# The first column block's sample tile: three products over 64 doubled columns, or two over high and low parts side by side

## The chip, the cores and the metric

The kernel runs on one core of one Trainium2 chip. The metric is the device time of one execution in microseconds (us). The engines are TensorE (PE, its weight loads PEld), VectorE (DVE), ScalarE (ACT), GpSimd (POOL) and SyncE (SP), which issues most transfers; ScalarE issues some too.

## The reference

One step of a decoder layer for 1024 prompt tokens and 64 sample tokens (8 sequences of 8), model width 1024. What matters here is its beginning, the normed input and the input projection, of which `gv` is one part of 768 columns:

```python
h = rmsnorm(x, norm_mix)
q, k, v, gu, gv, ga, gb = split_in(h @ w_in)
...
vn = layernorm(jax.nn.gelu(gv), ln_g, ln_b)
s = spatial_gating(jax.nn.gelu(gu), vn, ws, bs)
```

Attention, the gated merge, the ConvFFN and the final norm follow; the change leaves them alone. All tensors are float32.

## The kernel before

A float32 product is made of reduced-precision matmuls: each operand is split into a high part (a cast on ScalarE, or a scaled copy, L40 and L44) and a low part (the rest, on VectorE, L41 and L45), and a product is high x high + high x low + low x high, three matmuls into one PSUM bank.

The tokens lie in two groups. Group 0 has the 64 samples and the first 512 prompt tokens, 576 columns; group 1 the other 512. At the start, x of group 0 comes in 8 slices of 128 rows (k = 0 to 7, tiles `xk`, named `wh` and `wl` in the profile). `h_of` scales slice k by the norm's gain and splits it into `hs[k]`, a high and a low tile of 128x576. These lie in room that later belongs to the tiles `th` and `tl` of group 0, so the profile calls them so. The row's reciprocal root mean square is applied later, when PSUM is read: the squares of the slices (L637) are added up in `rs` (L639), the column sums come from five small matmuls (L476, in `stats`), and VectorE and GpSimd make the reciprocal root `rst` of them.

The weight blocks `gv0`, `gv1`, `v`, `gv2` are 256 columns wide, as `w2h` and `w2l`, with two buffers each: `v` can be cast only when `gv0` has been used. For `gv0` the five token tiles (samples, and four of 128 prompt tokens) have a PSUM bank each (`ps5`), and the loop runs over k outside and tiles inside, so that TensorE can start when the first slices have come. `mm_tok` makes a tile's three matmuls of one k: 128 token columns of `hs[k]` are the stationary operand, 256 weight columns the moving one. The sample tile takes columns 0 to 127 as well, of which only the first 64 are samples.

For the later blocks the sample tile is made otherwise. GpSimd copies the 64 sample columns of the high and of the low part of each k side by side into `pair_s` (L645), 128 columns, and two matmuls per k (L597) give high x w in rows 0 to 63 of the bank and low x w in rows 64 to 127. `joined` then copies the lower half to SBUF on ScalarE (L538) and adds the upper half on VectorE (L539). `gv_out` applies gelu with the row scale and stores the result; the `tokens` function runs a block and does one job of other preparation behind each tile.

A scheduler orders the instructions of each engine when the program is built; it takes the code's order and its own estimate of when each operand is there. What stands in the trace is that order. The names in it carry a buffer's number: `st_290` is the sample tile's bank of `gv0`, `st_291` to `st_294` the other four, `th3_249` holds `pair_s`.

Of the kernel before, what the change touches and what calls it, by code (L numbers as in the profile page):

```python
# [15 lines left out]
P = 128  # L16
D = 1024
KD = 8
# [16 lines left out]
def layer(tc, a):  # L35
# [11 lines left out]
    with ExitStack() as top:  # L47
# [311 lines left out]
        with ExitStack() as ph1:  # L359
# [158 lines left out]
            def h_of(k, x):  # L518
                hh, hl = rows576[2 * k], rows576[2 * k + 1]
                for s in (slice(0, 320), slice(320, 576)) if k == 0 else (slice(0, 576),):  # L520
                    scale_split(hh[:, s], hl[:, s], x[:, s], gains[:, 0, k:k + 1])
                hs.append((hh, hl))
# [5 lines left out]
            def mm_tok(ps, g, lo, w, k):  # L528
                wh, wl = w
                ah, al = ((part1(t, k, lo) for t in txa[1][k % 4]) if g else (t[:, lo:lo + P] for t in hs[k]))  # L530
                for i, (u, v) in enumerate(((ah, wh), (ah, wl), (al, wh))):
                    PE.matmul(ps, u, v[:, k, :], start=k + i == 0,  # L532
                              stop=k == KD - 1 and i == 2)

            def joined(ps):

                t = gvp.tile([P, 256], F32, name="gv")[0:NS]
                S.copy(t, ps[NS:P])  # L538
                V.tensor_add(t, t, ps[0:NS])  # L539
                return t  # L540
# [35 lines left out]
            def gv_out(g, i, p3, ps, v=None):  # L576
                name = groups[g]["toks"][i][0]
                m = NS if name == "s" else P
                if name == "s" and p3:
                    v = ps = joined(ps)  # L580
                elif v is None:
                    v = gvp.tile([P, 256], F32, name="gv")
                S.activation(v[0:m], ps[0:m], AF.Gelu_apprx_tanh, scale=1.0 if g else rstg[g][0:m, i:i + 1])
                nc.scalar.dma_start(gvd[name][0:m, 256 * p3:256 * p3 + 256], v[0:m])

            def tokens(g, key, out, jobs, new=True, after=None):
                if new:
                    W.get()
                    W.get()
                for i, (name, lo) in enumerate(groups[g]["toks"]):  # L590
                    ps = bank()[:, :256]
                    for k in range(KD):
                        if name != "s":
                            mm_tok(ps, g, lo, wide[key], k)
                            continue
                        for e in range(2):
                            PE.matmul(ps, pair_s[:, k], wide[key][e][:, k, :], start=k + e == 0,  # L597
                                      stop=k == KD - 1 and e == 1)
                    if after and i == 0:
                        after()  # L600
                    out(i, ps)
                    if jobs:
                        jobs.pop(0)()
# [18 lines left out]
                PE.matmul(ps[:, 0:P], ones, ones, start=True, stop=True)  # L622
            bank5 = [bank() for _ in toks0]
            ps5 = [x[:, :256] for x in bank5]
            W.split_part(0, 0, 2)
            for k, x in enumerate(xk):
                h_of(k, x)
                for part in ([(1, 0, 2)], [(0, 2, 4), (1, 2, 4)], [],
                             [(0, 4, KD), (1, 4, KD)], [], [], [], [])[k]:
                    W.split_part(*part)  # L630
                for kx in () if k == 0 else (0, 1) if k == 1 else (k,):
                    for i, (_, lo) in enumerate(toks0):
                        mm_tok(ps5[i], 0, lo, wide["gv0"], kx)
            W.load(5)
            W.emit(4)
            for k, x in enumerate(xk):
# [2 lines left out]
                    V.tensor_add(rsg[0], xk[0] if k == 1 else rsg[0], x)  # L639
            with tc.issue_after(dma.ins):  # L640
                load_late()
            pair_s = txa[0][3][0].rearrange("p j c -> p (j c)")[:, 0:KD * P].rearrange("p (k c) -> p k c", c=P)
            for k, x in enumerate(hs):
                for e in range(2):
                    G.tensor_copy(pair_s[:, k, 64 * e:64 * e + 64], x[e][:, 0:NS])  # L645
            rows, first_gv = {}, []

            def stats_first():
# [1408 lines left out]
```

## Time and profile before

| | |
|---|---|
| time, median of 3 runs | 1507.48 us (1507.39 to 1508.54) |
| profiled execution | 1506.67 us, span 1504.8 us |
| TensorE | 1491.9 us busy, 99% of the span, 12166 matmul records |
| VectorE, ScalarE, GpSimd | 77%, 55%, 19% of the span |
| granted TensorE clock | 0.998 |

A row of the timeline gives start, length, engine, line, operation, what it writes and reads, shapes, a count, and in brackets how long the engine was idle before it and what ended that. TensorE's matmuls overlap, and the profile models their ends: the pace is read from the starts. A weight load (PEld) that waits for its operand shows as a gap between two loads.

### The profile page before, as it was taken

To read this page: it belongs to the slowest core of one execution; us is meant where nothing else is said; L and a number is where in the kernel's file an instruction comes from. 1 tells how busy PE (TensorE), PEld (TensorE's weight loads), DVE (VectorE), ACT (ScalarE), POOL (GpSimd) and SP (SyncE) were. 2 spreads that over 40 slices of the span, in tenths; PEclk is the share of its full clock that TensorE was granted. 3 is DMA by queue.
4 is the path that set the end of the run, shared out by engine and by line. 5 is a ranking of instruction groups with operands and counts; after the bars stand their busy time and mean duration, and the time that the engine had idled before them with its cause. 6 is when DMAs were issued, how large, how long until landed. Compare 5 with 4: busy or idle time off the path is not lost.

```text
span 1504.8 us, 31429 instructions
## 1 busy us (share of the span) xinstructions
PE 1491.9 (99%) x12166; PEld 1478.9 (98%) x12166; DVE 1160.2 (77%) x1956; ACT 833.0 (55%) x1802; POOL 279.8 (19%) x438
## 2 busy tenths in 40 slices
PE   9999999999999999999999999999999999999997
PEld 9999999999999999999999999999999999999997
DVE  6877779656545996989678888898898888785675
ACT  7656764454553874864444655655555556453563
POOL 2001003101020332430223222232142122000002
PEclk9999999999999999999999999999999999999999
DMA  8552558547659757859978433332332317973454
GB/s 282 178 191 94 177 198 281 182 156 262 223 183 329 250 185 222 254 178 316 338 244 279 139 113 116 123 119 99 110 126 106 103 64 236 369 242 98 129 176 134
DMA packets 136868, 286.10 MB, mean 190 GB/s; under 512 B 15248, under 2 KB 43792, under 8 KB 136720
## 3 DMA queue, kind: packets, MB, share of 16 engines
q1 hardware_dynamic: 131904, 279.57, 55.7%
q10 hardware_dynamic: 4816, 4.54, 0.9%
q8 instruction: 95, 1.56, 0.4%
q14 instruction: 53, 0.43, 0.1%
HBM read 195.56 MB, written 90.46 MB: 190 GB/s over the span
## 4 chain that ended last, share of the span: by engine, by line
PE 91%; DVE 4%; ACT 1%; DMA 1%; issue 1%; SPq 0%; DVEq 0%; ACTq 0%
PE st L301 52%; PE dn L1796 15%; PE mm L241 14%; PE st L532 6%; PE sc L1289 1%; PE mx L898 1%; PE po L1350 1%; DVE s L1315 1%; DVE nm L1305 1%; DVE s L1299 1%; DMA wraw<-wt 1%; ACT s L1312 1%; DMA q<-qd 0%; PE pt L1322 0%; DVE wl L41 0%
## 5 line engine op out<-in xcount | busy, mean ns | idle before, releaser
L301 PE MATMUL st<-th,wh 128*128 128x256 f32 (+1 forms) x2128 | 610.4, 287 | 0.3 <-ACT k L282 0.2
L301 PE MATMUL st<-tl,wh 128*128 128x256 f32 (+1 forms) x2128 | 608.5, 286 | 0.0
L301 PE MATMUL st<-th,wl 128*128 128x256 f32 (+1 forms) x2128 | 608.1, 286 | 0.0
L301 PEld LDWEIGHTS st<-th,wh 128*128 128x128 f32 x2128 | 399.9, 188 | 1.6 <-ACT k L282 0.9
L301 PEld LDWEIGHTS st<-th,wl 128*128 128x128 f32 x2128 | 400.2, 188 | 0.0
L301 PEld LDWEIGHTS st<-tl,wh 128*128 128x128 f32 x2128 | 399.7, 188 | 0.0
L40 ACT CAST wh<-wraw 128x512 fp32r<-128x512 f32 (+1 forms) x244 | 144.1, 611 | 87.3 <-PE st L301 33.1
L41 DVE TENSOR_TENSOR wl<-wraw,wh 128x512 fp32r<-128x512 f32 (+1 forms) x244 | 165.2, 693 | 32.6 <-ACT wh L40 30.8
L1796 PE MATMUL dn<-th,wh 128*128 128x288 f32 (+1 forms) x616 | 176.7, 287 | 0.0
L1796 PE MATMUL dn<-tl,wh 128*128 128x288 f32 (+1 forms) x616 | 176.2, 286 | 0.0
L1796 PE MATMUL dn<-th,wl 128*128 128x288 f32 (+1 forms) x616 | 175.1, 284 | 0.0
L40 ACT CAST wh<-ws 128x512 fp32r<-128x512 f32 x160 | 98.1, 622 | 97.0 <-PE st L301 70.7
L41 DVE TENSOR_TENSOR wl<-ws,wh 128x512 fp32r<-128x512 f32 x160 | 109.2, 695 | 49.3 <-ACT wh L40 47.8
L1796 PEld LDWEIGHTS dn<-th,wl 128*128 128x128 f32 x616 | 115.9, 188 | 0.0
L1796 PEld LDWEIGHTS dn<-tl,wh 128*128 128x128 f32 x616 | 115.7, 188 | 0.0
L1796 PEld LDWEIGHTS dn<-th,wh 128*128 128x128 f32 x616 | 115.6, 188 | 0.0
L289 POOL TENSOR_TENSOR z<-ku,k 128x256 f32<-128x256 f32 (+1 forms) x32 | 30.9, 969 | 317.3 <-ACT ku L284 240.8
L40 ACT CAST th<-traw 128x544 fp32r<-128x544 f32 (+1 forms) x85 | 54.0, 642 | 48.4 <-PE dn L1796 36.6
L41 DVE TENSOR_TENSOR tl<-traw,th 128x544 fp32r<-128x544 f32 (+1 forms) x85 | 61.3, 728 | 21.8 <-ACT th L40 21.6
L241 PE MATMUL mm<-s,wh 128*128 128x256 f32 (+1 forms) x384 | 76.6, 294 | 0.1
L282 ACT COPY k<-st 128x256 f32<-128x256 f32 (+1 forms) x152 | 56.0, 382 | 34.8 <-PE st L301 33.9
L241 PE MATMUL mm<-oh,wh 128*128 128x256 f32 (+1 forms) x256 | 73.4, 287 | 0.1
(310 smaller groups left out, 3185.0 us busy)
## 6 DMA issues: line engine op xcount, KB each, us to landing
wraw<-wt SPq DMA_DIRECT2D x133, 512.0 KB
traw<-td SPq DMA_DIRECT2D x77, 272.0 KB
td<-za SPq DMA_DIRECT2D x22, 544.0 KB
wraw<-wt SPq DMA_DIRECT2D x35, 256.0 KB
upd<-hl SPq DMA_DIRECT2D x14, 512.0 KB
td<-t SPq DMA_DIRECT2D x11, 544.0 KB
qd<-q SPq DMA_DIRECT2D x8, 576.0 KB
q<-qd SPq DMA_DIRECT2D x8, 576.0 KB
```

The lines of the kernel that those rows point to most:

```text
L40: S.copy(hi, src)
L41: V.tensor_sub(lo, src, hi.bitcast(F32))
L241: PE.matmul(ps[:, lo:lo + c1 - c0], u[:, k, :], v[:, c0:c1], start=(clear and k == 0 and i == 0), stop=(k == nk - 1 and i == 2), skip_grou ...
L282: S.copy(t, src)
L289: op(to, pick(x, to, lo, hi), pick(y, to, lo, hi))
L301: PE.matmul(ps, u[:, kk, :], v, start=first and kk + i == 0, stop=kk == 3 and i == 2, skip_group_check=True)
L532: PE.matmul(ps, u, v[:, k, :], start=k + i == 0, stop=k == KD - 1 and i == 2)
L898: PE.matmul(ps[:, P * i:P * i + P], vn[:, i], late["wst"][:, c, :], start=True, stop=True)
L1289: PE.matmul(ps[:, h, o0:256], q, kst[kv][:, e, k0:cur + P], start=e == 0, stop=e == 1)
L1299: V.copy_predicated(s[:, :, 0:P], late["mprev"].to_broadcast([P, 4, P]), ps[:, :, 0:P])
L1305: V.tensor_reduce(nm, s, AX.X, ALU.max, negate=True)
L1796: PE.matmul(place(m, e), u[:, m, :], v[:, lo:hi], start=new and i + k == 0 and (e == 0 or m % 2 == 0), stop=i == NU - 1 and k == 2, skip_g ...
```

## The change

The sample tile of `gv0` is made like those of the later blocks. The copies into `pair_s` move from behind the whole block into the loop over k, right behind `h_of`. In the loop the four prompt tiles of a k come first and the sample tile last, by two matmuls over `pair_s` instead of three over `hs`. `gv_out` joins the halves for `gv0`, too. The two matmuls have a function of their own, which `tokens` uses as well.

```diff
+            def mm_s(ps, w, k):
+                for e in range(2):
+                    PE.matmul(ps, pair_s[:, k], w[e][:, k, :], start=k + e == 0, stop=k == KD - 1 and e == 1)
...
-                if name == "s" and p3:
+                if name == "s":
                     v = ps = joined(ps)
...
+            pair_s = txa[0][3][0].rearrange("p j c -> p (j c)")[:, 0:KD * P].rearrange("p (k c) -> p k c", c=P)
             W.split_part(0, 0, 2)
             for k, x in enumerate(xk):
                 h_of(k, x)
+                for e in range(2):
+                    G.tensor_copy(pair_s[:, k, 64 * e:64 * e + 64], hs[k][e][:, 0:NS])
...
-                    for i, (_, lo) in enumerate(toks0):
-                        mm_tok(ps5[i], 0, lo, wide["gv0"], kx)
+                    for i, (name, lo) in enumerate(toks0):
+                        if name != "s":
+                            mm_tok(ps5[i], 0, lo, wide["gv0"], kx)
+                    mm_s(ps5[0], wide["gv0"], kx)
...
-            pair_s = txa[0][3][0].rearrange("p j c -> p (j c)")[:, 0:KD * P].rearrange("p (k c) -> p k c", c=P)
-            for k, x in enumerate(hs):
-                for e in range(2):
-                    G.tensor_copy(pair_s[:, k, 64 * e:64 * e + 64], x[e][:, 0:NS])
```

TensorE at the end of k = 5 of `gv0`, before (`st_290` is the sample tile; `w2h_261` and `w2l_262` are gv0's weights, `tl1_242` holds the slice of k = 5, `th2_245` that of k = 6):

```order
L532 MATMUL st_293<-w2h_261,tl1_242 128x256
L532 MATMUL st_294<-w2h_261,tl1_242 128x256
L532 MATMUL st_294<-w2l_262,tl1_242 128x256
L532 MATMUL st_294<-w2h_261,tl1_242 128x256
L532 MATMUL st_290<-w2h_261,th2_245 128x256
L532 MATMUL st_290<-w2l_262,th2_245 128x256
```

and in the changed kernel:

```order
L532 MATMUL st_293<-w2h_261,tl1_242 128x256
L532 MATMUL st_294<-w2h_261,tl1_242 128x256
L532 MATMUL st_294<-w2l_262,tl1_242 128x256
L532 MATMUL st_294<-w2h_261,tl1_242 128x256
L537 MATMUL st_290<-w2h_261,th3_249 128x256
L537 MATMUL st_290<-w2l_262,th3_249 128x256
L532 MATMUL st_291<-w2h_261,th2_245 128x256
```

The sample tile stands at the end of each k and reads GpSimd's copy. GpSimd's own order of copies is the same in both kernels.

VectorE behind its last split of x, before (`w2l_452` are gv1's low weights, `w2l_519` those of `v`, `rs0_217` the sum of squares):

```order
L639 TENSOR_TENSOR rs0_217<-rs0_217,wl_258 128x576
L41 TENSOR_TENSOR w2l_452<-wraw_445,w2h_451 128x8x128
L41 TENSOR_TENSOR w2l_452<-wraw_447,w2h_451 128x8x128
L639 TENSOR_TENSOR rs0_217<-rs0_217,wh_259 128x576
L639 TENSOR_TENSOR rs0_217<-rs0_217,wl_260 128x576
L41 TENSOR_TENSOR w2l_519<-wraw_449,w2h_518 128x8x128
```

and in the changed kernel, where gv1's low weights are `w2l_460`, those of `v` `w2l_511`:

```order
L646 TENSOR_TENSOR rs0_217<-rs0_217,wl_258 128x576
L41 TENSOR_TENSOR w2l_460<-wraw_453,w2h_459 128x8x128
L41 TENSOR_TENSOR w2l_460<-wraw_455,w2h_459 128x8x128
L646 TENSOR_TENSOR rs0_217<-rs0_217,wh_259 128x576
L41 TENSOR_TENSOR w2l_511<-wraw_457,w2h_510 128x8x128
L646 TENSOR_TENSOR rs0_217<-rs0_217,wl_260 128x576
```

The last addition to the sum of squares now stands behind the first half of the low weights of `v`.

TensorE from the last sample matmuls of `gv0` on, in the changed kernel (`st_518` is gv1's sample tile, `st_571` its first prompt tile); before, the 16 sample matmuls of gv1 stood together, L476 right behind them and the first prompt tile behind L476:

```order
L537 MATMUL st_290<-w2h_261,th3_249 128x256
L537 MATMUL st_290<-w2l_262,th3_249 128x256
L537 MATMUL st_518<-w2h_459,th3_249 128x256
L532 MATMUL st_571<-w2h_459,th0_237 128x256
L537 MATMUL st_518<-w2l_460,th3_249 128x256
L537 MATMUL st_518<-w2h_459,th3_249 128x256
```

One matmul of the first prompt tile now stands ahead of gv1's first low product; behind the rest of the sample tile come six more of it, and then L476. Later differences in the order lie before about 90 us and move single instructions of preparation by a place or two; behind them the orders are the same.

More of the change, by code (lines that the diff above doesn't have):

```diff
@@ L592, in tokens @@
                     for k in range(KD):
-                        if name != "s":
+                        if name == "s":
+                            mm_s(ps, wide[key], k)
+                        else:
                             mm_tok(ps, g, lo, wide[key], k)
-                            continue
-                        for e in range(2):
-                            PE.matmul(ps, pair_s[:, k], wide[key][e][:, k, :], start=k + e == 0,
-                                      stop=k == KD - 1 and e == 1)
                     if after and i == 0:
@@ L641, in layer @@
                 load_late()
-            pair_s = txa[0][3][0].rearrange("p j c -> p (j c)")[:, 0:KD * P].rearrange("p (k c) -> p k c", c=P)
-            for k, x in enumerate(hs):
-                for e in range(2):
-                    G.tensor_copy(pair_s[:, k, 64 * e:64 * e + 64], x[e][:, 0:NS])
             rows, first_gv = {}, []
```

## The prediction

> **What bounds the kernel now.** I read the page first (busy shares, then the chain), then the chain over the first 80 us, then TensorE's weight loads, GpSimd, VectorE and ScalarE row by row up to 37 us, because the order of instructions differs only up to about 90 us.
>
> ```profile
> span 1504.8 us, 31429 instructions
> PE 1491.9 (99%) x12166; PEld 1478.9 (98%) x12166; DVE 1160.2 (77%) x1956; ACT 833.0 (55%) x1802; POOL 279.8 (19%) x438
> PE 91%; DVE 4%; ACT 1%; DMA 1%; issue 1%; SPq 0%; DVEq 0%; ACTq 0%
> ```
>
> TensorE is busy for 99% of the span and makes 91% of the chain, so a matmul less is time less unless TensorE then waits for data. The chain in the stage of the change (start, length, what):
>
> ```profile
> 9.88 0.88 DVE tl L45
> 10.75 0.04 issue
> 10.80 10.15 PE st L532 x85
> 20.95 2.00 PE st L597 x16
> 22.95 1.01 PE st L476 x10
> ```
>
> Up to 10.79 us TensorE is fed by ScalarE and VectorE, which split x and the weights; whatever is saved before that is waited off there. From 10.80 on TensorE is the chain: 85 matmuls of gv0, the 16 of gv1's sample tile (L597), the five column sums of squares (L476). The same stretch in TensorE's weight loads, each one step ahead of its matmul (start, length), and two matmuls for the pace:
>
> ```profile
> 10.79 0.30 PEld L532 LDWEIGHTS st<-w2h,tl 128*128 128x128 f32 x2 [0.26 <-DVE tl L45]
> 13.88 0.19 PEld L532 LDWEIGHTS st<-w2h,th 128*128 128x128 f32 x1
> 14.21 0.19 PEld L532 LDWEIGHTS st<-w2h,tl 128*128 128x128 f32 x1
> 20.68 0.19 PEld L597 LDWEIGHTS st<-w2h,th 128*128 128x128 f32 x1
> 20.98 0.19 PEld L597 LDWEIGHTS st<-w2l,th 128*128 128x128 f32 x1
> 22.68 1.20 PEld L476 LDWEIGHTS st<-c_ones,rs 128*128 128x128 f32 x10
> 23.79 0.19 PEld L532 LDWEIGHTS st<-w2h,th 128*128 128x128 f32 x1
> ...
> 17.39 0.28 PE L532 MATMUL st<-w2h,th 128*128 128x256 f32 x1
> 20.79 0.28 PE L597 MATMUL st<-w2h,th 128*128 128x256 f32 x1
> ```
>
> Between 17.39 and 20.79 lie exactly 30 matmuls (k = 6 and 7): 3.40 / 30 = 0.1135 us each, the price of a matmul. The step 13.88 to 14.21 is 0.33 instead of 0.11: 0.22 lost to the low part of k = 4. The step 20.68 to 20.98 is 0.30: 0.19 lost to gv1's low weights. So before, 0.41 us of waits lie on this path.
>
> **The change, part by part.**
>
> Removed: one of three matmuls for each of 8 k in gv0's sample tile, 8 x 0.1135 = 0.91 us of TensorE. The order has 35 matmuls of gv0 ahead of the wait at 10.79 both before and after (two k's tiles save two matmuls, and two more high-part matmuls of k = 2 go ahead of the wait), so all eight come off behind it.
>
> Added wait: the sample tile's matmuls of step k now wait for GpSimd's two copies of that k, which before were read only from 20.68 on. The copies themselves stand in the same order and behind the same producers, so I take their times from the trace (by the order of tiles: k = 2 low, k = 3 low, k = 4 low, k = 5 high, k = 6 high, k = 5 low, k = 7 low; first an undisturbed one):
>
> ```profile
> 9.90 0.24 POOL L645 CAST th<-tl 128x64 fp32r<-128x64 f32 x1 [1.50 <-ACT tl L44]
> ...
> 10.81 0.64 POOL L645 CAST th<-tl 128x64 fp32r<-128x64 f32 x1 [0.67 <-DVE tl L45]
> 12.14 0.74 POOL L645 CAST th<-th 128x64 fp32r<-128x64 f32 x1
> 14.22 0.71 POOL L645 CAST th<-tl 128x64 fp32r<-128x64 f32 x1 [0.69 <-DVE tl L45]
> 14.87 0.78 POOL L645 CAST th<-tl 128x64 fp32r<-128x64 f32 x1
> 15.60 0.78 POOL L645 CAST th<-th 128x64 fp32r<-128x64 f32 x1
> 16.33 0.78 POOL L645 CAST th<-tl 128x64 fp32r<-128x64 f32 x1
> 17.95 0.77 POOL L645 CAST th<-tl 128x64 fp32r<-128x64 f32 x1
> ...
> 14.75 0.81 DVE L45 SCALAR_TENSOR_TENSOR tl<-wl,c_gains,tl 128x576 fp32r<-128x576 f32 x1
> 15.48 0.81 DVE L45 SCALAR_TENSOR_TENSOR th<-wh,c_gains,th 128x576 fp32r<-128x576 f32 x1
> 16.21 0.81 DVE L45 SCALAR_TENSOR_TENSOR tl<-wl,c_gains,th 128x576 fp32r<-128x576 f32 x1
> ```
>
> A copy takes 0.24 with VectorE idle and 0.64 to 0.78 beside VectorE's splits. From 14.22 on GpSimd has no gap, and the order puts k = 6's high part before k = 5's low part, so the latter ends only at 16.33 + 0.78 = 17.11. Now I walk TensorE through the new order from 10.79, with 0.05 us from a producer's end to the load (VectorE's chain piece ends at 10.76, the load starts at 10.79; the row of gv1's weights below ends at 20.92, the load starts at 20.98):
> - k = 2: 5 matmuls, natural 11.36; the copy ends 11.45, load at 11.50: wait 0.14. Two matmuls: 11.73.
> - k = 3: 12 matmuls to 13.09, the copy is there at 12.88: none; two more, 13.32.
> - k = 4: 7 matmuls to 14.11; the low part at 14.21 as before: wait 0.10. Five: 14.78; the copy ends 14.93, load 14.98: wait 0.20. Two: 15.21.
> - k = 5: 12 matmuls to 16.57; the copy ends 17.11, load 17.16: wait 0.59. Two: 17.39.
> - k = 6 and 7: 28 matmuls without a wait (k = 7's copy ends 18.72): 20.57.
>
> Three waits for GpSimd, 0.93 in all. If each copy cost 0.24 they would be zero; if all came later by one more of GpSimd's 0.78 slots they would be about 1.7. I take 0.93, because nothing ahead of the copies changes.
>
> On this the Trainium skill has a rule (SBUF — State Buffer, section Who interferes with whom): VectorE with two inputs in SBUF and GpSimd reading SBUF exclude each other for the whole instruction, the later one is fully blocked. The trace agrees: copies end at 15.65, 16.38 and 17.11, 0.09 behind the ends of the three VectorE rows (15.56, 16.29, 17.02). By that rule the copies keep these times, and the sum is the one below; by the undisturbed 0.24 it would be 0.44 less.
>
> Next, gv1's start and the statistics. The new order on TensorE: gv1's first sample matmul, one matmul of tile 0, then the low weights; 15 more; six more of tile 0; then L476. On VectorE the third wide weight split goes ahead of the last addition of squares, which L476 reads:
>
> ```profile
> 19.71 1.21 DVE L41 TENSOR_TENSOR w2l<-wraw,w2h 128x1024 fp32r<-128x1024 f32 x1
> 20.85 0.75 DVE L639 TENSOR_TENSOR rs<-rs,wh 128x576 f32<-128x576 f32 x1
> 21.70 0.76 DVE L639 TENSOR_TENSOR rs<-rs,wl 128x576 f32<-128x576 f32 x1
> 22.38 1.22 DVE L41 TENSOR_TENSOR w2l<-wraw,w2h 128x1024 fp32r<-128x1024 f32 x1
> 20.99 1.05 ACT L40 CAST w2h<-wraw 128x1024 fp32r<-128x1024 f32 x1 [1.43 <-PE st L532]
> ```
>
> gv1's low weights (the first row) still end at 20.92: TensorE, there at 20.79, loads at 20.98: wait 0.19, as before. The cast that the split needs waits for gv0's last matmul (one step ahead of 20.79, so 20.67, and 0.32 to the cast's 20.99); now 20.57 + 0.32 = 20.89, end 21.94; the split runs from 21.99 to 23.21, the addition from about 23.14 to 23.90, L476 loads at 23.95. TensorE is there at 20.98 + 21 x 0.1135 = 23.36: wait 0.59, where before there was none. Were the addition in its old place it would be 0; with gv0's end unhindered the split would start at 21.60 and the wait be 0.15.
>
> Added besides: ScalarE's copy and VectorE's addition that join the two halves (the present ones of gv1):
>
> ```profile
> 22.99 0.37 ACT L538 COPY gv<-st 64x256 f32<-64x256 f32 x1 [0.95 <-PE st L597]
> 24.08 0.40 DVE L539 TENSOR_TENSOR gv<-gv,st 64x256 f32<-64x256 f32 x1
> 25.46 0.25 DVE L485 TENSOR_SCALAR stg<-c_ident,rst 64x64 f32<-64x64 f32 x1 [0.98 <-POOL rst L259]
> ```
>
> The copy fits into ScalarE's 0.95 of idle time, the addition into VectorE's 0.98: 0, and 0.77 if both covers were gone. The store orders moved on SP's queue near 70 us cost 0: in the waits of the whole run TensorE waits for a transfer only here,
>
> ```profile
> PE sc L1289 <- DMA q<-qd: 0.3, 1, 0.3
> ```
>
> and these are not it.
>
> Everything behind the statistics (reciprocal root, gelu, casts) is 23.95 + 1.11 - 23.79 = 1.27 later. First reader on TensorE that could notice is v's sample tile:
>
> ```profile
> 32.81 1.04 ACT L40 CAST w2h<-wraw 128x1024 fp32r<-128x1024 f32 x1
> 33.88 1.23 DVE L41 TENSOR_TENSOR w2l<-wraw,w2h 128x1024 fp32r<-128x1024 f32 x1 [0.25 <-ACT w2h L40]
> 36.17 0.19 PEld L597 LDWEIGHTS st<-w2h,th 128*128 128x128 f32 x1
> ```
>
> Its split ends at 35.11 + 1.27 = 36.38, TensorE is there at 36.17 + 0.49 = 36.66: 0.28 to spare, cost 0.
>
> The sum: -0.91, plus waits of 0.93 + 0.10 + 0.19 + 0.59 = 1.81 in place of 0.41: **+0.49 us**. The profiled execution took 1506.67 (1504.8 of span), so 1507.2 there; it lies 0.81 under the median of the runs, 1507.48, and on that median the forecast is **1508.0**.
>
> **The rivals.**
> - The saving shows. For it: the copies' rows are called rough by the page, and a semaphore may come earlier than the modelled end. Without GpSimd's waits the statistics wait falls to 0.15: the sum is +0.04 at 1507.5. With no new wait at all it is -0.91 at 1506.6. Against: 17.11 agrees with VectorE's own rows, and 20.92 and the order on VectorE are no matter of GpSimd.
> - The late statistics reach the weights of v. It decides where the delay passes 1.27 + 0.28 = 1.55 us: each further us is one of TensorE. With a delay of twice 1.27, 0.99 more: 1509.0; with three times, 2.26 more: 1510.2. For it: ScalarE's queue also issues the stores there. Against: TensorE's own delay moves with it.
> - Slower by more than can be overlooked: GpSimd sets the pace of gv0. From 10.81 to 18.72 lie 11 copies, 0.72 each. If the new matmuls on their tile slowed them to twice that, the last would end at 10.81 + 15.8 = 26.6, TensorE some 6.3 later than 20.34: 1514. It passes 3.0 us in sum from about 1.09 a copy. Against: the same queue, with the same VectorE work beside it, and TensorE read other tiles then without a trace on it.
> - The change does not remove the matmuls: excluded, the order has 8 fewer.
>
> **How the numbers follow.** The three runs of before spread over 1.15 us; 0.2% is 3.0 us, about what a measurement of this kernel can tell from no change. Chances: the forecast with its own range of 1507.4 to 1508.7, 0.55; the saving shows, 0.26; the late statistics, 0.13, a tenth of it beyond 3 us; GpSimd's pace, 0.03; something unthought-of 0.03, mostly faster. Faster 0.03, same 0.93, slower 0.04. The range leaves out some 2 in 10: from the full saving at 1506.5 to 1509.2, a doubled delay.
>
> **What would show it.** In the profile after: TensorE loads waiting for GpSimd near 11.4, 14.8 and 16.6 us, the longest about 0.6; gv0's last matmul near 20.6, 0.1 earlier than before; L476 waiting 0.6 for VectorE's addition near 23.9; the second token tile of gv1 starting 0.5 later than before; no new wait behind it. The forecast is wrong if gv0 ends before 20.2, if L476 starts before 23.5, or if v's sample tile waits.

## The result and the profile after

| | before | after |
|---|---|---|
| median of 22 runs (range) | 1508.38 us (1506.75 to 1512.22) | 1511.55 us (1505.41 to 1514.49) |
| ratio to before | | 1.0016 [1.0009, 1.0023] |
| two further comparisons of the same two kernels | | 1.0002 [0.9993, 1.0011], 0.9999 [0.9990, 1.0009] |
| profiled execution | 1506.67 us, span 1504.8 us | 1511.76 us, span 1510.0 us |

The eight matmuls are gone and the kernel is not faster. The forecast was 1508.0, range 1506.5 to 1509.2; the time of the first comparison, 1511.55, lies 2.35 us above that range. The other two comparisons gave medians of 1509.69 and 1507.21. The kernel before, run beside the first comparison, had 1508.38, which is 0.90 above the 1507.48 that the forecast was added to; against it the loss is 3.17 by the medians and 2.4 by the ratio, where the forecast had 0.49. Three executions were slow and are in no ratio: one of c_before (1615.47 us), one of e_allst2 (3542.61) and one of the kernel before beside e_all (1616.37). Where the time goes has two parts: a local loss in the first 48 us, and a pace of TensorE that differs from one execution to the next. Both are shown below.

The page of the kernel after:

```profile
PE 1496.1 (99%) x12158; PEld 1483.2 (98%) x12158; DVE 1161.9 (77%) x1957; ACT 832.9 (55%) x1803; POOL 279.3 (18%) x438
...
PE 93%; DVE 4%; ACT 1%; DMA 1%; issue 1%; SPq 0%; POOL 0%; DVEq 0%; ACTq 0%
```

Eight matmul records fewer, but 4.2 us more of TensorE's busy time. The chain of work of the kernel after, at gv0's end, the statistics and v (start, length, what):

```profile
20.58 0.13 PE st L537
20.73 1.06 ACT w2h L40
21.81 0.04 DVE w2l L41
22.95 0.76 DVE rs L646
23.76 1.28 PE st L476 x10
```

The chain leaves TensorE for the cast of gv1's weights, the split behind it and the addition of squares that now stands behind that split, and comes back at L476: the forecast's path, with a wait of 0.36 instead of 0.59. The waits of TensorE's weight loads between 10 and 60 us of the kernel after (total us, number, longest) are two:

```profile
PEld st L493 <- ACT stg L483: 0.7, 2, 0.4
PEld st L476 <- DVE rs L646: 0.4, 1, 0.4
```

The first of them the forecast does not have. The weight loads themselves, of the kernel after and then of the kernel before:

```profile
20.53 0.19 PEld L537 LDWEIGHTS st<-w2h,th 128*128 128x128 f32 x1
23.76 1.19 PEld L476 LDWEIGHTS st<-c_ones,rs 128*128 128x128 f32 x10 [0.36 <-DVE rs L646]
36.80 0.19 PEld L537 LDWEIGHTS st<-w2h,th 128*128 128x128 f32 x1
45.28 0.30 PEld L493 LDWEIGHTS st<-stg,c_ones 128*128 128x128 f32 x2
45.88 0.59 PEld L493 LDWEIGHTS st<-stg,c_ones 128*128 128x128 f32 x4 [0.30 <-ACT stg L483]
46.86 0.30 PEld L493 LDWEIGHTS st<-stg,c_ones 128*128 128x128 f32 x2 [0.39 <-ACT stg L483]
```

```profile
44.42 1.02 PEld L493 LDWEIGHTS st<-stg,c_ones 128*128 128x128 f32 x8
```

L493 is the matmul that spreads group 1's row scales over the partitions; its eight loads took 1.02 before, and now 1.88 (45.28 to 47.16), in three pieces. The first starts without a wait, the second and the third wait for a diagonal tile that ScalarE writes (L483).

To place the losses I took the start of the same matmul (counted from the end of the program, since both kernels have the same ones there) and subtracted its start in the first profile of before (the other execution of before is c_before of the experiments, the 2nd and 3rd profile of after are c_after and c_after2):

| us later than before, at about | 24 | 27 | 35 | 48 | 64 | 124 | 440 | 860 | 1260 | 1480 us |
|---|---|---|---|---|---|---|---|---|---|---|
| before, another execution | .15 | .15 | .15 | .11 | .11 | -.10 | -.29 | -.48 | -.62 | 2.57 |
| after, 1st profile | .20 | .34 | .58 | 1.72 | 1.72 | 1.75 | 1.43 | 1.38 | 1.62 | 4.51 |
| after, 2nd | .12 | .18 | .18 | 1.85 | 1.22 | -.27 | -.45 | -.52 | -.62 | -.53 |
| after, 3rd | .17 | .24 | .24 | 1.47 | .84 | .93 | .61 | .20 | .10 | .19 |

At 35 us, where the forecast says +0.49, stand +0.58, +0.18 and +0.24. By 48 us all three have lost 1.5 to 1.9 us. In the second that is 0.18, a wait of 0.74 at v's sample tile (below), and 0.86 at L493 (1.88 instead of 1.02), 1.78 in sum of 1.85. (The first has no wait at v: 0.86 at L493 and 0.58 before it, and most of the rest is a slower pace of TensorE.) Then the rows part: one execution gives all of it back, one half, and one keeps it and loses 2.9 more behind 1260 us. Even two executions of the kernel before lie 2.6 us apart at the end.

The last loss has no wait in it. The window from 1300 to 1460 us, of before and of after (stretch, its length, then busy time and count of PE, PEld, DVE, ACT, POOL, then granted clock, DMA share, GB/s):

```profile
1300.00:1460.00 160.00, 160.00 (x1308) 160.00 (x1307) 113.29 (x204) 75.84 (x139) 0.00 (x0) 1.00 0.58 184
```

```profile
1300.00:1460.00 160.00, 160.00 (x1287) 160.00 (x1286) 112.83 (x201) 73.81 (x134) 0.00 (x0) 1.00 0.58 188
```

and of the third profile of after:

```profile
1300.00:1460.00 160.00, 160.00 (x1307) 160.00 (x1306) 113.10 (x204) 75.79 (x138) 0.00 (x0) 1.00 0.58 184
```

TensorE is busy throughout at the same granted clock of 1.00, and does 1308 or 1287 matmuls in the same 160 us. Between 60 and 100 us it does 342 in before and in the first profile of after, and 349 in the third. The median step from one 256-column matmul to the next is 113 ns in some stretches and 118 ns in others, and one pace holds for tens of microseconds or longer. Before has 113 up to 40 us, 118 from there to 120, 118 once more in parts of the stretch from 480 to 760, and 113 at the end. The first profile of after has 118 from 23 to 120 and again from 1297 to 1460; both of these changes stand at a pause of TensorE (a step of 0.44 us at 23.3, one of 0.31 at 1297.4), but the change of before at 40 us stands at none. The second and third have 113 in most of the stretch from 48 to 100 us, where before has 118, and so come back. The other execution of before (c_before) has 118 from 1260 us on, so the slow end is not the change's own.

Now the local loss. Two chains were not in the forecast. The first is ScalarE's queue: gv0's stores are issued there, ahead of v's sample scaling (L676; L673 before) and the cast of v's second half. ScalarE's rows of the kernel after, then of before (ACTq is an issue of a transfer):

```profile
31.77 0.33 ACTq L588 DMA_DIRECT2D gvd<-wl  x1
32.69 0.63 ACT L676 ACTIVATE stg<-wh 128x512 f32<-128x512 f32 x1 [2.12 <-DMA gvd<-wl]
34.11 1.04 ACT L40 CAST w2h<-wraw 128x1024 fp32r<-128x1024 f32 x1
```

```profile
29.60 0.33 ACTq L584 DMA_DIRECT2D gvd<-wl  x1
31.39 0.63 ACT L673 ACTIVATE stg<-wh 128x512 f32<-128x512 f32 x1 [1.70 <-DMA gvd<-wl]
```

The cast is at 34.11 instead of 32.81. The squares' late sum is part of that: the first gelu, the first user of the statistics, starts at 26.53 instead of 25.46. But from the end of the gelus on, what ScalarE waits for is the landing of another store. Transfers signal their end on eight semaphores that the scheduler deals out in turn, and gv0's last store shares one with gv0's first: it may not be issued before that one has landed. The first lands late if SP has put weight loads ahead of it: where SP does so, the last store is issued 4.7 to 8.7 us after the first (eight profiles here), where SP does not, 3.0 to 3.6 us after it (seven). SP's rows, before and after:

```profile
24.92 0.33 SPq L146 DMA_DIRECT2D wraw<-wt  x1
...
29.89 1.43 SPq L146 DMA_DIRECT2D wraw<-wt  x2
```

```profile
23.84 1.72 SPq L146 DMA_DIRECT2D wraw<-wt  x3
```

Before, the second of three weight loads (512 KB each) stood at 29.89; now all three go out from 23.84 on. The order of SP's instructions with their waits tells why; each of before, then of after:

```
32 L146 DMA wraw<-wt 128x1024 [waits DMAHW0_49]
32 L146 DMA wraw<-wt 128x1024 [waits DMAHW7_49]
```

Number 0 had been dealt to the store of gv0's first prompt tile, whose landing ended SP's wait at 29.89; now gv1's sample store has it, and the weight load got number 7, last used by a load of x that had long landed. One reordered store shifted the deal, and a load that had been held back by chance went free. That the issuing queue stands is in accord with the Trainium skill (DMA: Bandwidth & Descriptors, section "Anatomy of one DMA — SWDGE (gpsimd) path"): DMA engines do not wait on semaphores, the wait is on the issuing sequencer before dispatch. It does not bear on which transfers share one; only the rows show that.

### The profile page after: what moved, and what is told of

It reads as the page before. It is cut to its first block, busy times and chain, and to the rows that moved or that the text cites. A ratio compares the mean times of both kernels' runs of the same rounds, so it can differ in the third digit from the quotient of the medians.

```text
span 1510.0 us, 31417 instructions
## 1 busy us (share of the span) xinstructions
PE 1496.1 (99%) x12158; PEld 1483.2 (98%) x12158; DVE 1161.9 (77%) x1957; ACT 832.9 (55%) x1803; POOL 279.3 (18%) x438
## 4 chain that ended last, share of the span: by engine, by line
PE 93%; DVE 4%; ACT 1%; DMA 1%; issue 1%; SPq 0%; POOL 0%; DVEq 0%; ACTq 0%
PE st L301 51%; PE dn L1799 15%; PE mm L241 14%; PE st L532 6%; PE sc L1292 1%; PE po L1353 1%; PE mx L901 1%; PE pt L1325 1%; ACT s L1315 1%; DVE nm L1308 0%; DMA q<-qd 0%; DMA wraw<-wt 0%; DVE s L1318 0%; DVE of L1364 0%; DVE s L1302 0%
## 5 line engine op out<-in xcount | busy, mean ns | idle before, releaser
L241 PE MATMUL mm<-oh,wl 128*128 128x256 f32 (+1 forms) x256 | 73.6, 288 | 0.0
```

Of the source, the lines that this page charges most:

```text
L241: PE.matmul(ps[:, lo:lo + c1 - c0], u[:, k, :], v[:, c0:c1], start=(clear and k == 0 and i == 0), stop=(k == nk - 1 and i == 2), skip_grou ...
```

## The experiments

Each kernel ran in 11 or 12 executions beside the kernel before (e_hold and b_more in 5, e_hold2, b_pad and e_hold64 in 6); the ratio with its 95% interval is to that. The central numbers first: weight loads that SP issued from 23 to 28 us, issue of gv0's last store, cast of v's second half, wait at v's sample tile on TensorE, delay at 48 us (as in the table above).

| kernel | loads | store | cast | v's wait | at 48 us | ratio |
|---|---|---|---|---|---|---|
| before | 1 | 29.60 | 32.81 | 0 | 0 | |
| after, 1st to 3rd | 3 | 31.77, 32.51, 31.76 | 34.11, 34.94, 34.55 | 0, 0.74, 0.29 | 1.72, 1.85, 1.47 | 1.0016, 1.0002, 0.9999 |
| e_rst | 3 | 33.03 | 35.40 | 0.71 | 1.98 | 1.0005 [0.9996, 1.0013] |
| e_sq | 3 | 33.08 | 35.80 | 1.07 | 2.87 | 1.0008 [0.9998, 1.0019] |
| e_diag | 3 | 33.75 | 36.30 | 0.24 + 1.07 | 2.56 | 1.0011 [1.0001, 1.0022] |
| e_all | 3 | 33.61 | 35.96 | 0.94 + 1.07 | 2.54 | 1.0018 [1.0007, 1.0029] |
| b_free (on before) | 4 | 34.70 | 36.49 | 1.23 + 1.07 | 3.25 | 1.0012 [1.0003, 1.0021] |
| e_hold | 1 | 30.46 | 34.01 | 0 | 2.14 | 1.0054 [1.0042, 1.0067] |
| e_store | 1 | elsewhere | 32.27 | 0 | 0.18 | 0.9997 [0.9986, 1.0008] |
| e_allst | 1 | elsewhere | 31.21 | 0 | -0.02 | 0.9990 [0.9981, 0.9998] |

**The two kernels again** (c_after and c_before are the same code as after and before).

> The changed kernel once more. Theory A (the loss is two waits in the first 50 us, the rest is a matmul pace that is drawn anew in each execution): L476 again waits some 0.36 us for VectorE's last addition of squares, group 1's L493 again some 0.7 us in two pieces for ScalarE; at 60 us the changed kernel is 1.1 to 1.8 us behind; the pace of the 256-column matmuls from 1300 us on may be 113 or 118 ns, and the ratio to before lies between 1.0005 and 1.002. Theory B (the change makes the slow pace of the last stage its own): 118 ns again from 1300 us on, and the ratio again near 1.002.

> The kernel before once more, as a control. Both theories: ratio 1.000 within 0.001. Theory A: stages with a 256-column pace of 113 and of 118 ns stand partly in other places than in the first profile, the last stage perhaps at 118. Theory B: 113 ns from 1300 us on again.

c_after: 1509.69 us, 1.0002 (expected was 1.0005 or more); c_before: 1507.88, 0.9997 [0.9988, 1.0006]. The kernel after again had no slow stage at the end, while c_before had one, against the theory that the change makes it. The local loss came again (1.85), and v's tile now waited, which it had not in the first profile:

```profile
37.28 0.19 PEld L537 LDWEIGHTS st<-w2l,th 128*128 128x128 f32 x1 [0.74 <-DVE w2l L41]
```

In the first profile the cast was 0.83 earlier (34.11 against 34.94) and TensorE 0.40 later, at the pace of 118 from 23 us on, so v's weights were just there. They are 1.3 to 2.1 later than before in all three executions; whether TensorE sees it depends on both.

**Group 1's reciprocal root, and the order of the squares.** In the kernel after, the first step of group 1's root (L258) goes ahead of the split of gv2's weights on VectorE, and GpSimd's power behind it (L259) then runs beside that split. GpSimd and VectorE of the kernel after, then GpSimd of before:

```profile
42.85 1.94 POOL L259 TENSOR_TENSOR rst<-rst,c_eps 128x4 f32<-128x4 f32 x1 [16.36 <-DVE rst L258]
```

```profile
42.69 1.23 DVE L41 TENSOR_TENSOR w2l<-wraw,w2h 128x1024 fp32r<-128x1024 f32 x1
```

```profile
42.76 1.02 POOL L259 TENSOR_TENSOR rst<-rst,c_eps 128x4 f32<-128x4 f32 x1 [17.34 <-DVE rst L258]
```

The same instruction takes 1.02 without the split and 1.94 beside it; it ends at 44.79, 0.87 behind the split's end at 43.92. That agrees with the Trainium skill (SBUF — State Buffer, section "Who interferes with whom"), by which a VectorE instruction with two SBUF inputs and a GpSimd one that reads SBUF exclude each other. e_rst puts L258 behind the split; e_sq puts the last square addition ahead of v's first split, as before.

```diff
 # e_rst
+                with tc.issue_after(W.low.ins) if g else ExitStack():
                     rroot(rstg[g], pt)
 # e_sq, where gv1 is fetched; late["sq"] is the last addition into rs
+                with tc.issue_after(late["sq"].ins):
                     W.get(); W.get()
```

> The changed kernel with one order restored: VectorE's root of group 1's statistics (L258) stands behind the second half of the low weights of gv2 again, as in the kernel before. Theory A: GpSimd's power takes 1.0 us again instead of 1.94, ScalarE writes the four diagonal blocks in a row, L493 waits 0.2 us or less instead of 0.7, and at 60 us the kernel is 0.7 to 1.0 us ahead of the changed one; in the ratio 0.0006 less than the changed kernel, which the interval may not show. Theory B: the last stage keeps 118 ns and the ratio stays at 1.002.

> The changed kernel with the other order restored: VectorE's last addition of squares stands ahead of the first half of the low weights of v again. Theory A: L476 waits for nothing, 0.3 to 0.4 us less on TensorE by 27 us; everything behind the statistics comes about 1 us earlier, so L493 of group 1, whose order is left, may wait a little less than 0.7. Theory B: no change of the ratio, 1.002, and 118 ns in the last stage.

e_rst: the power is back at 1.02 and L493 waits 0.3 instead of 0.7; e_sq: L476 no longer waits. Both repairs worked where they were made, and neither won: 1509.23 and 1509.25, with a loss at 48 us of 1.98 and 2.87, more than the 1.5 to 1.9 of the kernel after. In both, v's tile waits (0.71 and 1.07). If late statistics alone were the reason for v's wait, as the rival of the prediction had it, e_sq, whose first gelu starts at 26.16 instead of 26.53, should have a shorter one; its wait is the longer.

**Which part of group 1's wait is whose.** e_diag leaves L258 early and puts only ScalarE's four diagonal writes behind v's sample scaling; e_all restores all three orders.

```diff
 # e_diag, where the diagonal tiles are written; late["vs"] is v's sample scaling
+                with tc.issue_after(late["vs"].ins) if g else ExitStack():
                     S.activation(dg[...], ident...)
```

> The changed kernel with ScalarE's four diagonal writes of group 1 behind the scaling of v's sample tile, as before; VectorE keeps the reciprocal root's first step ahead of gv2's second half split, so that GpSimd's power of it runs beside that split. If GpSimd's power is what L493 waits for: the power takes 1.9 us again instead of 1.0, and L493 waits 0.6 us or more in all. If ScalarE's order is: the power takes 1.9, too, but L493 waits at most 0.35. v's sample tile waits 0.7 or more in either case.

> The changed kernel with three orders put back as they were before: the last two additions of squares ahead of v's first low split, and in group 1 the first step of the reciprocal root (L258) behind gv2's low split, and the four diagonal writes behind the scaling of v's sample tile. Theory (the store blocks ScalarE): the waits for the squares (L476) and at group 1's L493 go (under 0.1 and at most 0.35 us), but v's sample tile still waits 0.7 to 1.1 us, because ScalarE still stands behind the store of gv0's last tile; TensorE at 47.8 us is 1.2 to 2.0 us later than before. Rival (the orders alone make every wait): v's sample tile waits at most 0.1, and TensorE at 47.8 us is 0.4 to 1.0 later than before. Time: within 1506 to 1512 under both, because the pace of TensorE moves more than this.

GpSimd's power in e_diag:

```profile
44.58 1.94 POOL L259 TENSOR_TENSOR rst<-rst,c_eps 128x4 f32<-128x4 f32 x1 [17.63 <-DVE rst L258]
```

It is as slow as in the kernel after, yet L493 has no wait in that kernel. ScalarE's rows of the kernel after show what is different there: two other jobs stand between the four diagonal writes, and the two waits of L493 are for the writes behind them.

```profile
44.82 0.40 ACT L483 ACTIVATE stg<-c_ident,rst 128x128 f32<-128x128 f32 x1 [2.52 <-POOL rst L259]
45.13 0.39 ACT L40 CAST ws<-gv 128x256 fp32r<-128x256 f32 x1
45.43 0.69 ACT L483 ACTIVATE stg<-c_ident,rst 128x128 f32<-128x128 f32 x2
46.02 0.49 ACT L550 ACTIVATE gv<-gv,rst 64x256 f32<-64x256 f32 x1
46.42 0.39 ACT L483 ACTIVATE stg<-c_ident,rst 128x128 f32<-128x128 f32 x1
```

So the 0.7 at L493 is ScalarE's order. That the slow power costs nothing is not shown: in e_diag TensorE had waited 1.31 at v and came to L493 the later. With the writes in a row, L493 still waited 0.3 at its start in e_rst and 0.5 in e_all (0.35 at most was expected), because the writes then start only behind the power, which ends at 45.97 and 46.53.

e_all settles the rival of the late statistics. Its rows on ScalarE and on TensorE's loads:

```profile
25.43 0.48 ACT L592 ACTIVATE wl<-st,rst 128x256 f32<-128x256 f32 x1 [1.56 <-POOL rst L259]
...
33.61 0.33 ACTq L593 DMA_DIRECT2D gvd<-wl  x1
34.54 0.63 ACT L685 ACTIVATE stg<-wh 128x512 f32<-128x512 f32 x1 [4.82 <-DMA gvds<-gv]
```

```profile
37.04 0.19 PEld L542 LDWEIGHTS st<-w2h,th 128*128 128x128 f32 x1 [0.94 <-ACT w2h L40]
38.30 0.19 PEld L542 LDWEIGHTS st<-w2l,th 128*128 128x128 f32 x1 [1.07 <-DVE w2l L41]
```

The first gelu starts at 25.43, against 25.46 before: nothing is late. Still ScalarE stands 4.82 for the landing of a store, and v waits 2.01, more than the 0.7 to 1.1 expected. Of the kernels so far it has the highest ratio, 1.0018, but not by v's wait alone: at 101 and 103 us its loads wait another 0.58 and 1.89 for a weight block, where before has no such wait (e_diag: 1.82 at 101 us). Why these come is open.

**The two stores on another queue.** If ScalarE's standing is the cause, it goes when the two stores in question (gv0's last tile, gv1's samples) are issued by GpSimd.

```diff
-                    nc.scalar.dma_start(gvd[...], v[0:m])
+                    (nc.gpsimd if (g, p3, name) in ((0, 0, 3), (0, 1, "s")) else nc.scalar).dma_start(gvd[...], v[0:m])
```

> The changed kernel, but two stores leave ScalarE's queue for GpSimd's: that of gv0's last tile, which waits for the landing of gv0's sample store, and that of gv1's sample tile. Theory (the store blocks ScalarE): no wait of ScalarE of over 2 us ahead of L676, the cast of v's second half starts before 34.0 us, and v's sample tile waits at most 0.15 us instead of 0.7; TensorE at 47.8 us is 0.5 to 1.2 us later than before instead of 1.85. Rival (v's weights are late because the statistics or the weights' own transfer are): v's sample tile still waits 0.5 us or more, 1.5 to 2.2 at 47.8 us. The wait for the squares stays, some 0.4.

> All of it together: the changed kernel with the three orders put back and the two stores on GpSimd's queue. Theory: TensorE waits for GpSimd's copies (0.5 to 1.0 in sum) and nowhere else up to 60 us; at 47.8 us it is 0.0 to 0.6 later than before. Rival (something not yet seen): a wait of over 0.3 us remains at L476, v's sample tile or L493. By time it can be the fastest version, by up to 1 us, which is less than the pace of TensorE moves it.

> The kernel before with the two stores of the version above on GpSimd's queue (gv0's last tile and gv1's sample tile): a control, which tells what moving them is worth without the change. Theory: no wait in the kernel before came from them, so the same, within 0.1%, and TensorE at 47.8 us within 0.2 of before. Rival (the gain of the version with everything together came from the stores): 1 us or more faster.

> The version with everything together once more, to see whether its gain stands: by the matmuls saved and the waits left (0.91 less, some 0.2 to 0.6 of waits for GpSimd more) 0.3 to 0.7 us faster than before at 47.8 us when the pace is the same in both profiles, and 0.03 to 0.1% by the runs; if the first result was the pace of TensorE alone, the interval holds 1.000.

e_store is the changed kernel with that alone: v's wait is gone and the cast stands at 32.27. Its first gelu is as late as in the kernel after (26.48), so late statistics alone do not make v wait. L493's wait went too, which I had not aimed at; I take it that with v early ScalarE's other jobs are done by then, but no run shows that by itself. Its delay at 48 us is 0.18, where 0.5 to 1.2 was expected, and the runs give 0.9997. e_allst, with the three orders too: -0.02 at 48 us, 0.9990, and 0.9996 [0.9987, 1.0005] the second time. b_store is the control, the stores of the kernel before moved in the same way: 1.0001 [0.9989, 1.0013], so they win nothing by themselves. But moving the stores changes the deal of semaphores as well (the table: SP's loads are held back again), so this pair does not tell ScalarE's standing from SP's early loads.

**The loads alone.** e_hold adds one small load (2 KB) to the changed kernel, so that the semaphores fall as before and SP's second weight load is held back again; ScalarE's stores stay. b_free does the reverse to the kernel before: gv1's sample store alone goes to GpSimd, and the weight load goes free.

```diff
 # e_hold, ahead of the loads of the statistics' inputs
+                nc.sync.dma_start(c1.tile([P, NKV], F32, name="c_more0"), a["sinks"])
 # b_free
-                    nc.scalar.dma_start(gvd[...], v[0:m])
+                    (nc.gpsimd if (g, p3, name) == (0, 1, "s") else nc.scalar).dma_start(gvd[...], v[0:m])
```

> The changed kernel with one more load of 2 KB on SP's queue. Through it the scheduler deals the queue's completion semaphores out differently: v's second half of weights, as in the kernel before, again shares one with the store of gv0's first prompt tile and so waits for its landing (in the changed kernel it waits for a load that is long done). ScalarE's queue and its order around the stores stay as in the changed kernel. Theory (the weight loads that go ahead fill the transfer engines, and the stores land behind them): only one weight load is issued between 23 and 28 us instead of three, gv0's last tile is stored before 30.8 us instead of after 31.7, v's cast starts before 33.8 and v's sample tile waits at most 0.2 us. Rival (the stores land late because they are issued a microsecond late): the store at 31.5 or later, and v's sample tile waits 0.5 us or more.

> The reverse, on the kernel before: only gv1's sample store moves to GpSimd's queue. By that the semaphore that it had becomes free for v's second half of weights, which no longer waits for the store of gv0's first prompt tile; the statistics, the sample tile of three products and the stores of gv0 stay. Theory: three weight loads go out between 23 and 28 us, gv0's last tile is stored after 31.5 us instead of 29.6, and v's sample tile waits 0.5 to 2 us for its weights, so that TensorE at 47.8 us is 0.5 to 2 us later than in the kernel before, with none of the change in it. Rival (it needs the late statistics or the moved tile): the store before 30.5, no wait for v's weights.

Rows of b_free, SP, then ScalarE, then TensorE's loads at v:

```profile
23.86 2.40 SPq L146 DMA_DIRECT2D wraw<-wt  x4
```

```profile
34.70 0.33 ACTq L584 DMA_DIRECT2D gvd<-wl  x1
35.07 0.63 ACT L673 ACTIVATE stg<-wh 128x512 f32<-128x512 f32 x1 [4.56 <-DMA wraw<-wt]
```

```profile
37.57 0.19 PEld L597 LDWEIGHTS st<-w2h,th 128*128 128x128 f32 x1 [1.23 <-ACT w2h L40]
38.83 0.19 PEld L597 LDWEIGHTS st<-w2l,th 128*128 128x128 f32 x1 [1.07 <-DVE w2l L41]
```

This is the kernel before, with its sample tile by three products, its statistics in time and no wait for GpSimd, and it has the largest wait at v of all, 2.30, and 3.25 at 48 us (0.5 to 2 was expected for both). Four loads went out from 23.86 on, one more than in the kernel after, so it is not the exact reverse, and the size is not to be carried over. (The row puts ScalarE's wait down to a weight load; but gv0's last store is issued only at 34.70, 8.7 us after the first, and L673 follows it.) Of e_hold, SP, then ScalarE:

```profile
25.40 0.33 SPq L146 DMA_DIRECT2D wraw<-wt  x1
...
30.43 2.10 SPq L146 DMA_DIRECT2D wraw<-wt  x2
```

```profile
30.46 0.35 ACTq L588 DMA_DIRECT2D gvd<-wl  x1
...
34.01 1.04 ACT L40 CAST w2h<-wraw 128x1024 fp32r<-128x1024 f32 x1
```

With the load held back the store is issued at 30.46 and v does not wait (its 2.14 at 48 us are L493 and a slower pace from the start). TensorE came to v later there than in the kernel after (0.97 later than before at 35 us, by its pace), but not by this alone: the split of v ends at 36.31, and in c_after, which waits, TensorE was there at 36.54. The cast was expected at 33.8 at the latest; in the repetition, e_hold2, it is at 33.48. That is 0.67 to 1.20 later than before, which v can bear, and which late statistics and TensorE's pace make up between them; the kernel after has 1.30 to 2.13. Over all profiles, v's sample tile waits in seven of the eight with free loads, and in none of the twelve with the load held back (five of these have the stores moved as well). So the free loads make v's wait, with the change and without it. No run gives gv0's last store a semaphore of its own while the loads are free; that it is the shared one that holds ScalarE rests on the order of the waits and the rows. But e_hold lasted 1515.48 us, 0.54% longer, and the loss lies between 120 and 860 us, far behind the load (5.84 at 440, 8.83 at 860). That asked for an explanation of its own.

**Why a 2 KB load costs 8 us.** b_more puts such a load into the kernel before, with every instruction in its old order; e_hold2 is e_hold again; c_after2 is the changed kernel a third time.

```diff
 # b_more, in tokens between the two fetches for gv1
+                nc.sync.dma_start(c1.tile([P, NKV], F32, name="c_more0"), a["sinks"])
```

> The kernel before with one more load of 2 KB on SP's queue, of the same data as in the version that held the weight loads back; the order of all other instructions on every engine is that of before, and v's second half of weights still stands behind the store. If the extra load makes TensorE's pace slow: 3 us or more slower, pace 117 to 118 ns between 120 and 440 us. If not: the same within 0.1%, pace 113 there.

> The version that holds v's weight loads back, once more. If the slow pace belongs to this program: 1513 or more again, 117 ns between 120 and 440 us. If it was the draw of one session: 1506 to 1511. The waits in either case as before: none at v's sample tile, 0.4 for the squares, 0.7 at group 1's L493.

> The changed kernel a third time. By the waits alone (0.4 for the squares, 0 to 1.1 at v's sample tile, 0.7 at L493, against 0.91 saved) 0.7 to 1.9 us at 60 us; by the two comparisons so far 0.0 to 2.4 us over before. The more v's sample tile waits, the more often the pace behind it is 113 instead of 118 up to 120 us, which gives back up to 1.7 us.

b_more 1515.72, 1.0055 [1.0043, 1.0067]; e_hold2 1516.34, 1.0062 [1.0048, 1.0075]. So it is not the change, and not a rare execution. What the load brings is a tile of 16 bytes in the constants' pool, which moves some 800 of the 2360 tiles of the built program by 32 bytes (the weights' `w2h` from 131968 to 132000). b_pad has the tile without load and without use; e_hold64 has e_hold's load with a tile of 64 bytes, which moves the same ones by 64.

```diff
 # b_pad, on before
+            c1.tile([P, 4], F32, name="c_pad")
 # e_hold64
+                nc.sync.dma_start(c1.tile([P, 16], F32, name="c_more0")[:, 0:NKV], a["sinks"])
```

> The kernel before with a tile of 16 bytes a partition in the pool of constants that no instruction touches; no load more, and the order of all instructions that of before. If where the tiles lie sets the pace (32 bytes off): 117 ns between 120 and 440 us and 1513 or more, as with the load. If the load did it: the same as before, 113 ns.

> The version that holds v's weight loads back by one more 2 KB load, its tile now 64 bytes wide. If the tiles' place sets the pace: 113 ns between 120 and 440 us again and 1506 to 1511; waits as in that version: none at v's sample tile, 0.4 for the squares, 0.7 at L493, so 0.5 to 1.5 later than before at 47.8 us where the pace is the same. If the load does: 1513 or more.

b_pad 1513.38, 1.0038 [1.0023, 1.0052]: an unused tile costs 0.4%. Whether the load itself adds to that is open, since b_more's interval overlaps b_pad's. e_hold64 1519.08, 1.0074 [1.0061, 1.0087]: the expectation that 64 bytes would give the old pace back did not come true. The windows from 120 to 440 us of before, b_pad and e_hold64 (columns as above):

```profile
120.00:440.00 320.00, 320.00 (x2583) 319.63 (x2582) 215.72 (x358) 178.28 (x361) 44.18 (x52) 1.00 0.57 193
```

```profile
120.00:440.00 320.00, 320.00 (x2547) 319.77 (x2547) 212.94 (x354) 175.71 (x354) 39.90 (x45) 1.00 0.57 192
```

```profile
120.00:440.00 320.00, 320.00 (x2539) 319.77 (x2538) 214.27 (x357) 175.50 (x354) 39.39 (x39) 1.00 0.56 191
```

TensorE is busy throughout at a granted clock of 1.00 in all three, and does 2583, 2547 and 2539 matmuls. From 860 to 1460 us, where the tiles lie where they lay, all three have the same number but for three in 4883. The median step from 120 to 440 us is 114 ns in before, 117 with the 16-byte tile and 120 with the 64-byte one, and from 440 to 840 us it is 114, 117 and 119. So where the tiles lie changes the pace; why these places are slower is not settled, nor whether 117 is the 118 of above lasting longer. The ratio of e_hold says nothing about holding the loads back; its waits up to 40 us do.

**The version that the runs point to.** e_best is e_allst with GpSimd's copies in the order of k, so that TensorE does not wait for them.

```diff
+                    with tc.issue_after(late["copy"].ins) if k else ExitStack():
-                    G.tensor_copy(...)
+                        late["copy"] = G.tensor_copy(...)
```

> The version with everything together, and GpSimd's copies in the order of k, so that the low part of k = 5 no longer stands behind the high part of k = 6. By the sum: the wait for GpSimd of 0.5 goes, at 47.8 us 0.5 to 0.9 earlier than before where the pace is the same, by the runs 0.03 to 0.1% faster than before. If the copies' order doesn't matter: 0.0 to 0.5 earlier, as in the two runs without it.

Its only wait of TensorE's loads from 10 to 50 us is one for gv1's low weights:

```profile
PEld st L542 <- DVE w2l L41: 0.5, 1, 0.5
```

At 48 us it is 0.47 ahead of before, of the 0.91 that the change removes, and the runs give 1506.97 and 0.9994 [0.9984, 1.0004]. The three comparisons of the repaired kernels (0.9990, 0.9996, 0.9994) all lie below 1, by 0.6 to 1.5 us, only one with an interval that leaves 1 out. By the ratios at most 0.1% is to be had, by the lowest end of the intervals 0.2%.

## Why the prediction was right and wrong

- **Eight matmuls off, waited off before gv0 ends.** Right in size, by luck in the first profile: gv0's end (gv1's first sample load) is at 20.53 instead of 20.68, 0.15 earlier; the forecast had 0.11. But there the saving did not go into waits for GpSimd: the 36th load of gv0, which the forecast has at 10.79 in both kernels, is at 11.63, because TensorE started at 5.62 instead of 5.43 and had the full granted clock only from 9.98 on instead of 6.90. (By the rows that the prediction shows, the price of a matmul is 3.40 / 30 = 0.1133, not 0.1135; the eight come to 0.91 either way.)
- **Waits for GpSimd, 0.93.** Over-sized: 0 in the first and third profile, 0.53 at 16.93 in the second, beside one at 5.95 us. In the first and third TensorE got the full clock only at 9.98 and 10.06, and the copies were there in time; in the second it had it from 4.62 on.
- **L476 waits for the moved addition, 0.59.** Right in kind, 0.36, 0.47 and 0.36 in size. The delay up to there came out at 0.18 to 0.58 against 0.49.
- **"First reader on TensorE that could notice is v's sample tile ... 0.28 to spare, cost 0."** This step failed. It carried the statistics' delay of 1.27 forward to v's cast and split, as though nothing else stood there. The statistics' delay itself was near (the first gelu is 1.07 later), but the cast came 1.30 to 2.13 later, because ScalarE stood at a store, and v waited 0.74 and 0.29 in two of three executions. That it did not in the first, whose cast was 1.30 later, is luck: TensorE was late itself. The rival of the late statistics put the loss at the right place, and they have a share in the cast's delay (0.67 to 1.20 at most, by e_hold2 and e_hold), but they are not what makes v wait: e_all has the statistics in time and v waits 2.01, b_free has nothing of the change and v waits 2.30, e_store has them late and v waits for nothing.
- **"The store orders moved on SP's queue near 70 us cost 0."** True of those, and it was the wrong place to look: what counted was a weight load near 24 us that kept its place in the order and lost its wait.
- **"No new wait behind it."** Failed: L493 waits 0.7 in all three profiles and costs 0.86, since ScalarE's four diagonal writes were interleaved with other jobs. With v's wait this makes the local loss 1.5 to 1.9 instead of 0.49.
- **One price of a matmul, 0.1135, for the whole run.** Failed: the pace is 113 or 118 ns by stage and execution. The prediction had taken one stretch's pace for the whole, and its own range, 1507.4 to 1508.7, had no room for it. The profiled execution of after was 4.5 us behind that of before at 1480 us: 1.7 of it local, 2.9 by the pace behind 1260 us.
- **Faster, same, slower.** "Same" within 0.2% holds for all three ratios (the first one's interval reaches to 1.0023); the narrow range failed. Their mean excess is (3.17 + 1.54 - 0.44) / 3 = 1.4 us by the medians and 0.9 us by the ratios; with a pace that moves an execution by more than that, no run shows the local loss in the whole time. Why the first comparison came out at 1.0016 and the others at 1.000 stays open, and with it what part of 1511.55 is the change.

## What to carry to other kernels

Where a change reorders stores or loads, compare the waits of every transfer on the issuing queues in the two orders, not only their places: a deal of shared completion semaphores can free one load and block another engine's queue some ten microseconds on (8 to 11 here). A repair that shortens the wait one sees can lengthen one behind it, so take the delay of the same instruction at several points, not only at the end. And when differences of some tenths of a per cent matter, compare addresses and the step between matmuls first: a 16-byte tile that nothing uses cost more here than anything that the change did.

## What was not expected of the hardware

- TensorE's step between 256-column matmuls was either 113 or 118 ns in the kernels without a padding tile, at a granted clock of 1.00 and without a gap between them; the same program showed either in the same stage (before and c_before from 1300 us on).
- Moving a third of the tiles in SBUF by 32 bytes gave 117 ns, by 64 bytes (one kernel, with a load more) 120 ns, for some 700 us of the run; these kernels took 0.4 to 0.7% longer.
- A GpSimd instruction over 128x4 elements took 1.94 us instead of 1.02 beside VectorE's split of 1.23.
